# V turned by VectorE's 32x32 block transpose and read as strided weights, in a block of dilated attention and RG-LRU

## The chip, the core and the metric

The kernel runs on one core of a Trainium2 chip. Its engines work from queues of their own and wait for one another by semaphores: TensorE (PE; its weight loads are shown apart, as PEld), VectorE (DVE), ScalarE (ACT), GpSimd (POOL), and SyncE (SP), which issues most DMAs here. The metric is device time of one execution in microseconds (us), lower is better. Shown times are medians of several executions. The profile is of one execution.

## What is computed

One decoder block in float32, for 2048 positions and a model width of 1024. An input projection to 9216 columns feeds attention (24 heads of 64 in three groups with dilations 1, 4 and 16), a gated linear recurrence, and gates. The change concerns V, from the projection to the product of the attention weights with it:

```python
proj = x @ w_in[l] + b_in[l]
q, k, v, g_attn, u_lru, g_lru, gate_logits = jnp.split(proj, SPLIT_POINTS, axis=-1)
...
def to_blocks(t):          # positions regrouped by residue mod dilation, then blocks of 128
    t = t.reshape(B, M, dilation, H, Dh).transpose(0, 2, 1, 3, 4)
    return t.reshape(B, dilation, nb, BAND_BLOCK, H, Dh)
...
s = jnp.einsum('brnqhd,brnkhd->brnhqk', qb, kw) * (Dh ** -0.5)
...
p = jnp.exp(s - m)
o = jnp.einsum('brnhqk,brnkhd->brnqhd', p, vw)
```

A query block of 128 sees its own key block and the one before it; with dilation 16 there is one block for each residue. The results of the groups are combined, gated and projected, merged with the recurrence branch, projected again and normalised.

## The kernel before

The kernel has three stages, one after the other.

**Stage A, the projection.** The 72 column tiles of 128 are computed in pairs, each pair for one half of the positions at a time ("plan", 72 entries). Most pairs go through a scheme with seven block products instead of eight: `product(s, j)` (L622) issues 12 matmuls of 128x512 into one PSUM bank `q`, with weights split into a high part `h` and a low part `l`; `evacuate(s, j)` (L650) combines the banks on DVE, and `result` (L587) makes one 128x512 tile (128 columns of the projection by 512 positions, called chunk `c`) out of a bank and a partial sum. One product is one tick of the schedule. A loop over the ticks (L878) issues the product, the events due at this tick (weight loads, and the preparation of weights, four products ahead of their use in the first half of the plan and three in the second), and the next steps of "chains": generators that do what is left for one result tile, each step held back by `Ask` until a budget of engine time is there. The order on every engine is thus fixed when the program is built.

Twelve column tiles are V, for three groups `g` and four pairs of heads `hp`, so there are 48 tiles of V: 24 in the first half of the plan and 24 in the second. `v_chain` (L363) handles one tile. It lays positions on partitions: four 128x128 transposes on PE (`turn`, L367, tile `vtp`) are put into the middle of a later product, ACT copies the bank to `vs` and applies the sign that the seven-product scheme leaves on the second tile of a pair (L378), and SP stores it to DRAM (`v_scr`, L382 and L384). PSUM is divided into four banks `q`, two `t` for `vtp` and two `g` for the recurrence's gates.

**Stage B, the attention.** There are 12 units `u` (a pair of heads in a group; groups in the order 0, 2, 1). `qk_parts` and `v_parts` (L805) load a unit's q, k and V one unit ahead into one of two buffers; `v_parts` gives four parts of one 256 KB DMA each, with partition = key within its block. A loop runs over 48 groups of work, four for each unit: scores (L992, L998), softmax numerators on DVE and ACT (L1012, L1014), their transposes on PE (L1029), and `values` (L1046), whose matmuls (L1061) take 64 columns of V, one head, as weights. The two heads of a unit go to different halves of the output partitions, so they come in pairs. From the fifth group on, 12 matmuls of the recurrence's projection (L1231, tile `yb`) stand in each group; their weights `wl` and inputs `hx` are loaded by SP and split by POOL. DMAs on SP rotate over eight semaphores; an issue waits until the DMA eight places before it has landed.

**Stage C** is the two last projections and the layer norm.

The lines that matter below: L360 to L385 (`v_chain`), L583 (a result tile out of a bank), L630 (a product's bank), L670 (a partial sum), L805 to L822 (`v_parts`), L1046 to L1062 (`values`).

Of the kernel before, what the change touches and what calls it, by code (L numbers as in the profile page):

```python
# [15 lines left out]
P = 128  # L16
S = 2048
# [14 lines left out]
def hybrid_block_kernel(ctx: ExitStack, tc: tile.TileContext, a: dict, out: bass.AP):  # L32
# [16 lines left out]

    v_scr = [[dram.tile([S, P], F32, name=f"v_scr{g}{j}") for j in range(HP)] for g in range(3)]  # L50

# [307 lines left out]

    vs_free = [sl_p.tile([P, 520], F32, name=f"vs{j}")[:, 0:CH].rearrange("p (b f) -> p b f", b=4) for j in range(2)]  # L360
    tog = {"n": 0}

    def v_chain(vt, sgn, f, c):  # L363
        g, hp = divmod(f - FT_V, 4)
        st = {}

        def turn():  # L367
            tp = st["tp"] = ps.tile([P, 4, P], F32, tag="t", name=f"vtp{f}_{c}", bufs=2)
            for b in range(4):
                pe.transpose(tp[:, b, :], flat(vt)[:, b * P:(b + 1) * P], ident)  # L370
            give(vt)

        yield Ask(cond=lambda: tog["n"] < 2)
        tog["n"] += 1
        pe_later(2, turn)
        yield Ask(lag=3, cond=lambda: len(vs_free) > 0, ACT=.66)
        vs = vs_free.pop(0)
        act.activation(vs, st["tp"], AF.Copy, scale=sgn)  # L378
        tog["n"] -= 1
        yield Ask()  # L380
        if g == 0:
            sp.dma_start(v_scr[g][hp].rearrange("(p n) f -> p n f", p=P)[:, 4 * c:4 * c + 4], vs)  # L382
        else:
            sp.dma_start(v_scr[g][hp][c * CH:(c + 1) * CH].rearrange("(b p) f -> p b f", p=P), vs)  # L384
        vs_free.append(vs)  # L385

# [200 lines left out]
    def result(s, fi, c, bank, u):  # L587
# [34 lines left out]
    def product(s, j):  # L622
# [27 lines left out]
    def evacuate(s, j):  # L650
# [154 lines left out]
    def v_parts(u):  # L805
        g, hp = unit(u)
        src = v_scr[g][hp]

        def part(i):
            def fn():  # L810
                if u == 0 and i == 0:
                    AT_X["v"] = big("X4", [P, 2, 16, P], F32, "V")
                V = AT_X["v"][:, u % 2, 4 * i:4 * i + 4]
                if g == 0:
                    sp.dma_start(V, src.rearrange("(p n) f -> p n f", p=P)[:, 4 * i:4 * i + 4])
                elif g == 1:
                    sp.dma_start(V, src[i * CH:(i + 1) * CH].rearrange("(j r) f -> j r f", r=4))
# [228 lines left out]
    def values(js, tag="o"):  # L1046
        o = aps.tile([P, 4, P], F32, tag=tag, name=f"o{js[0]}", bufs=2 if tag == "s0" else 1)
        out = []
        for i, j in enumerate(js):
            u, n0 = divmod(2 * j, 16)  # L1050
            g, _ = unit(u)
            V = AT_X["v"][:, u % 2]
            ptb, _, los = st.pop(("t", j))
            for b in range(2):
# [3 lines left out]
                for x in range(lo // P, 2):  # L1058
                    kb = n if x else pv
                    for h, hs in enumerate((lo_, up_)):  # L1060
                        pe.matmul(o[hs, 2 * i + b, :], V[:, kb, 64 * h:64 * h + 64], ptb[:, b, 2 * h + x, :],  # L1061
                                  start=(x == lo // P), stop=(x == 1))  # L1062
# [598 lines left out]
```

## Time and profile before

| | us |
|---|---|
| median of 3 executions (2113.68 to 2114.83) | 2114.58 |
| span of the profiled execution | 2110.6 |
| stage A, until the last matmul of L639 | about 1451 |
| stage B, first score matmul to the last of L1061 | 1451 to 1774 |
| busy in the span: PE, PEld, DVE, ACT, POOL | 2092.4, 1713.1, 1645.0, 1212.7, 764.2 |

The span is from the first to the last instruction; a time of the table's first row holds some 4 us more, which lie around it. Busy time of PE counts matmuls that overlap once. In the views below a row of the timeline is: start in us, duration in us, engine, line, operation, output<-inputs, shapes, number of instructions merged, and in brackets the idle time before it with what ended it. A row of the groups has busy time in us, then the mean of one in ns, then idle time before it. A row of the windows has busy time for each engine with the number of instructions, the clock granted to TensorE, the mean busy share of the DMA engines and GB/s.

### The profile page before, as it was taken

Reading aid. Unit: us, or ns where it says so; the run is one execution under the profiler, and the core shown is the slowest. Engines: PE = TensorE matmul, PEld = TensorE weight load, DVE = VectorE, ACT = ScalarE, POOL = GpSimd, SP = SyncE. Lnnn points to the kernel's source line nnn. Section 1 sums busy time; section 2 is a strip of 40 time slices with the busy share of each in tenths; the row PEclk is TensorE's granted clock in tenths of the full one; section 3 lists DMA queues with packets and bytes.
Section 4 is the critical chain, followed back from the end, with each engine's and each line's share of the span. In section 5 each row is a group of like instructions: output and inputs, shape, how many; then the busy total and the mean of one; then the engine's idle time right before and its main releaser. Section 6 shows DMA issues by size and latency. Waiting matters only on the chain.

```text
span 2110.6 us, 35731 instructions
## 1 busy us (share of the span) xinstructions
PE 2092.4 (99%) x12069; PEld 1713.1 (81%) x12069; DVE 1645.0 (78%) x2937; ACT 1212.7 (57%) x2510; POOL 764.2 (36%) x685
## 2 busy tenths in 40 slices
PE   9999999999999999999999999999999999999998
PEld 7888888888888888888888888887888878788886
DVE  8878988989988868677777878875667776877667
ACT  6456556567567556677677787775666664321100
POOL 1544653653653301111111111112547678521120
PEclk9999999999999999999999999999999999999999
DMA  7876976886886866566665666669879886774431
GB/s 222 245 230 196 266 227 203 255 239 208 248 256 210 301 192 181 191 205 174 206 190 175 207 205 204 188 205 275 209 208 260 233 234 184 243 243 154 152 100 70
DMA packets 259205, 443.10 MB, mean 210 GB/s; under 512 B 65504, under 2 KB 92160, under 8 KB 255952
## 3 DMA queue, kind: packets, MB, share of 16 engines
q1 hardware_dynamic: 242384, 408.38, 62.0%
q0 software_dynamic: 11744, 23.54, 6.0%
q10 hardware_dynamic: 4896, 8.92, 1.1%
q8 instruction: 96, 1.57, 0.3%
q14 instruction: 85, 0.70, 0.1%
HBM read 289.74 MB, written 150.99 MB: 209 GB/s over the span
## 4 chain that ended last, share of the span: by engine, by line
PE 95%; DMA 2%; DVE 1%; POOL 1%; ACT 1%; issue 1%; SPq 0%; ACTq 0%; POOLq 0%; DVEq 0%
PE q L639 65%; PE yb L1231 6%; PE o L1061 3%; PE z L1536 3%; PE z L1537 3%; PE z L1538 3%; PE pt L1029 2%; PE s L998 2%; PE ya L1504 1%; PE ya L1503 1%; PE ya L1505 1%; PE g L500 1%; PE vtp L370 1%; PE s L992 1%; DMA war<-in_w_f_dram 1%
## 5 line engine op out<-in xcount | busy, mean ns | idle before, releaser
L639 PE MATMUL q<-xT,hS 128*128 128x512 f32 x1632 | 505.0, 391 | 0.1
L639 PE MATMUL q<-xT,l 128*128 128x512 f32 x1088 | 423.5, 389 | 0.0
L639 PE MATMUL q<-xB,hA 128*128 128x512 f32 x1344 | 418.0, 392 | 0.0
L639 PE MATMUL q<-xB,l 128*128 128x512 f32 x944 | 367.9, 390 | 0.0
L639 PEld LDWEIGHTS q<-xT,hS 128*128 128x128 f32 x1632 | 304.6, 188 | 65.0 <-issue 2.7
L639 PEld LDWEIGHTS q<-xB,hA 128*128 128x128 f32 x1344 | 250.7, 188 | 57.0 <-issue 5.8
L639 PEld LDWEIGHTS q<-xT,l 128*128 128x128 f32 x1088 | 204.3, 188 | 42.6
L240 POOL TENSOR_TENSOR sw<-sw,sin 128x512 f32<-128x512 f32 x96 | 156.8, 1639 | 166.2 <-ACT sw L329 94.7
L639 PEld LDWEIGHTS q<-xB,l 128*128 128x128 f32 x944 | 177.5, 188 | 37.2
L240 POOL TENSOR_TENSOR y<-y,h 128x512 f32<-128x512 f32 x28 | 38.8, 1386 | 384.1 <-DVE h L541 352.1
L1014 ACT ACTIVATE pb<-pb 128x192 f32<-128x192 f32 (+1 forms) x384 | 160.7, 422 | 26.5 <-DVE pb L1012 26.4
L639 PE MATMUL q<-xB,hS 128*128 128x512 f32 x544 | 169.0, 392 | 0.0
L639 PE MATMUL q<-xT,hA 128*128 128x512 f32 x544 | 167.8, 390 | 0.0
L284 ACT ACTIVATE hA<-wA 128x512 fp32r<-128x512 f32 x220 | 138.6, 636 | 28.5 <-DVE l L240 9.1
L1231 PE MATMUL yb<-hx,wl 128*128 128x512 f32 x576 | 148.9, 400 | 0.1
L284 ACT ACTIVATE hS<-S 128x512 fp32r<-128x512 f32 x170 | 108.6, 639 | 60.7 <-DVE S L240 47.3
L240 POOL TENSOR_TENSOR l<-wA,hA 128x512 fp32r<-128x512 f32 x68 | 107.8, 1585 | 91.4 <-ACT hA L284 60.9
L1231 PEld LDWEIGHTS yb<-hx,wl 128*128 128x128 f32 x576 | 104.8, 188 | 28.4 <-issue 5.6
L639 PEld LDWEIGHTS q<-xT,hA 128*128 128x128 f32 x544 | 101.9, 188 | 21.4 <-issue 0.4
L639 PEld LDWEIGHTS q<-xB,hS 128*128 128x128 f32 x544 | 101.2, 188 | 21.5 <-issue 1.1
L240 DVE TENSOR_TENSOR S<-S,wA 128x512 f32<-128x512 f32 x102 | 96.8, 949 | 11.5 <-DMA wA<-in_w_in_dram 7.9
L1507 POOL TENSOR_TENSOR me<-gA,me 128x512 f32<-128x512 f32 x30 | 47.7, 1607 | 157.6 <-DVE gA L1506 135.3
(213 smaller groups left out, 4325.4 us busy)
## 6 DMA issues: line engine op xcount, KB each, us to landing
wA<-in_w_in_dram SPq DMA_DIRECT2D x220, 256.0 KB
wl_scr<-l SPq DMA_DIRECT2D x102, 512.0 KB
l<-wl_scr SPq DMA_DIRECT2D x102, 512.0 KB
wS<-in_w_in_dram SPq DMA_DIRECT2D x102, 256.0 KB
wS<-in_w_in_dram POOLq DMA_DIRECT2D x68, 256.0 KB, 7.0
wlr<-in_w_f_dram SPq DMA_DIRECT2D x64, 256.0 KB
mg_scr<-y SPq DMA_DIRECT2D x59, 256.0 KB
v_scr<-vs SPq DMA_DIRECT2D x48, 256.0 KB
```

The source lines that it names most:

```text
L240: eng.tensor_tensor(out=out, in0=in0, in1=in1, op=op)
L284: act.activation(heads(h), heads(r, False), AF.Copy)
L639: pe.matmul(bank, w[:, ks], x[:, kk, xx], start=(first and i == 0), stop=(last and i == 11))
L998: pe.matmul(bank[h][es, b, 0:BW], q[hs, n * P + 64 * e:n * P + 64 * e + 64], k_[hs, at + 64 * e:at + 64 * e + BW], start=True, stop=True)
L1014: act.activation(pp, pp, AF.Exp, scale=-1.0, bias=mm, accum_out=ll)
L1029: pe.transpose(pt[e][:, b, 2 * h + x, :], pdata(p, h, c, c + P)[hs], ident[hs, hs])
L1061: pe.matmul(o[hs, 2 * i + b, :], V[:, kb, 64 * h:64 * h + 64], ptb[:, b, 2 * h + x, :], start=(x == lo // P), stop=(x == 1))
L1231: pe.matmul(YB["t"], w[:, a, k], hx(8 * c + k)[:, b], start=(hf == 0 and m == 0), stop=(hf == 1 and m == 11))
L1507: (dve if i in (6, 7) else pool).tensor_tensor(out=ME[c][:, f], in0=ga, in1=ME[c][:, f], op=ALU.add)
L1536: pe.matmul(z, mh[:, k], w[:, 0, hs], start=(k == 0), stop=False)
L1537: pe.matmul(z, mh[:, k], w[:, 1, hs], start=False, stop=False)
L1538: pe.matmul(z, ml[:, k], w[:, 0, hs], start=False, stop=(k == 7))
```

## The change

For a tile of V the four PE transposes, the PSUM bank and the ACT copy go. DVE turns the tile itself, with an instruction that transposes each 32x32 block; its operands are strided so that the positions of one block are those that belong together in the group's order. After it a partition stands for a quarter of the features and a position within its block, so `v_scr` gets another layout, `[4, 128, 512]`, and the load puts the quarters of the features side by side: `v_parts` now fills a quarter of V's partitions (32 keys of each block) at a time, with one DMA of 256 KB for a quarter in group 2, and four DMAs of 64 KB, with pieces of 512 bytes, in groups 0 and 1. The keys of a block then lie in V with a stride, of 64 bytes in group 2 and 16 bytes in the others, and `values` reads them so as weights. The sign that ACT applied is now put into the sums on DVE: for V pairs the partial sum `u3` is made with the other sign, and the result is bias + partial sum - bank. The two banks freed go to `q`, which has six. A buffer `vs` is given back two ticks later than before.

```diff
-    v_scr = [[dram.tile([S, P], F32, name=f"v_scr{g}{j}") for j in range(HP)] for g in range(3)]
+    v_scr = [[dram.tile([4, P, CH], F32, name=f"v_scr{g}{j}") for j in range(HP)] for g in range(3)]
...
-    def v_chain(vt, sgn, f, c):
+    def v_chain(vt, f, c):
+
         g, hp = divmod(f - FT_V, 4)
-        st = {}
-
-        def turn():
-            tp = st["tp"] = ps.tile([P, 4, P], F32, tag="t", name=f"vtp{f}_{c}", bufs=2)
-            for b in range(4):
-                pe.transpose(tp[:, b, :], flat(vt)[:, b * P:(b + 1) * P], ident)
-            give(vt)
-
-        yield Ask(cond=lambda: tog["n"] < 2)
-        tog["n"] += 1
-        pe_later(2, turn)
-        yield Ask(lag=3, cond=lambda: len(vs_free) > 0, ACT=.66)
+        y = flat(vt)
+        yield Ask(lag=0, cond=lambda: len(vs_free) > 0, DVE=.3)
         vs = vs_free.pop(0)
-        act.activation(vs, st["tp"], AF.Copy, scale=sgn)
-        tog["n"] -= 1
+        if g == 2:
+            dve.transpose(vs.rearrange("p (j r) -> p r j", r=16), y.rearrange("p (i r) -> p r i", r=16))
+        else:
+            src = y.rearrange("p (b q i) -> p q b i", q=4, b=4) if g == 0 else y.rearrange("p (q i b) -> p q b i", q=4, b=4)
+            dve.transpose(vs.rearrange("p (q j b) -> p q b j", q=4, b=4), src)
+        give(vt)
         yield Ask()
-        if g == 0:
-            sp.dma_start(v_scr[g][hp].rearrange("(p n) f -> p n f", p=P)[:, 4 * c:4 * c + 4], vs)
-        else:
-            sp.dma_start(v_scr[g][hp][c * CH:(c + 1) * CH].rearrange("(b p) f -> p b f", p=P), vs)
-        vs_free.append(vs)
+        if g == 2:
+            sp.dma_start(v_scr[g][hp][c], vs)
+        else:
+            sp.dma_start(v_scr[g][hp][:, :, P * c:P * c + P].rearrange("q p x -> p q x"), vs.rearrange("p (q x) -> p q x", q=4))
+        later(2, lambda: vs_free.append(vs))
...
-            total(flat(y), bank, u, f, sgn, True)
-            start_chain(qk_chain(y, f, c) if kind == "qk" else v_chain(y, sgn, f, c))
+            if kind == "v" and fi:
+                dve.scalar_tensor_tensor(out=flat(y), in0=u, scalar=b72[:, f:f + 1], in1=bank, op0=ALU.add, op1=ALU.subtract)
+            else:
+                total(flat(y), bank, u, f, sgn, True)
+            start_chain(qk_chain(y, f, c) if kind == "qk" else v_chain(y, f, c))
...
-            Q["b"] = ps.tile([P, CH], F32, tag="q", name=f"q{j}_{s}", bufs=4)
+            Q["b"] = ps.tile([P, CH], F32, tag="q", name=f"q{j}_{s}", bufs=6)
...
-            tt(dve, Q["u3"], Q["u2"], b, ALU.add)
+            if plan[s][4] == "v":
+                dve.scalar_tensor_tensor(out=Q["u3"], in0=b, scalar=-1.0, in1=Q["u2"], op0=ALU.mult, op1=ALU.subtract)
+            else:
+                tt(dve, Q["u3"], Q["u2"], b, ALU.add)
...
-        def part(i):
+        def part(q):
             def fn():
-                if u == 0 and i == 0:
-                    AT_X["v"] = big("X4", [P, 2, 16, P], F32, "V")
-                V = AT_X["v"][:, u % 2, 4 * i:4 * i + 4]
-                if g == 0:
-                    sp.dma_start(V, src.rearrange("(p n) f -> p n f", p=P)[:, 4 * i:4 * i + 4])
-                elif g == 1:
-                    sp.dma_start(V, src[i * CH:(i + 1) * CH].rearrange("(j r) f -> j r f", r=4))
+                if u == 0 and q == 0:
+                    AT_X["v"] = big("X4", [P, 2, 4, CH], F32, "V")
+                v = AT_X["v"][32 * q:32 * q + 32, u % 2]
+                m = src[q].rearrange("(a i) x -> i a x", a=4)
+                if g == 2:
+                    sp.dma_start(v, m)
                 else:
-                    sp.dma_start(V, src.rearrange("(i r) f -> i r f", r=16)[:, 4 * i:4 * i + 4])
+                    for c in range(4):
+                        sp.dma_start(v[:, c].rearrange("i (a x) -> i a x", a=4), m[:, :, P * c:P * c + P])
             return fn
...
             V = AT_X["v"][:, u % 2]
+            V = V.rearrange("p a (j r) -> p r (a j)", r=16) if g == 2 else V.rearrange("p c (f b) -> p c b f", b=4)
...
-                        pe.matmul(o[hs, 2 * i + b, :], V[:, kb, 64 * h:64 * h + 64], ptb[:, b, 2 * h + x, :],
+                        pe.matmul(o[hs, 2 * i + b, :], (V[:, kb] if g == 2 else V[:, kb // 4, kb % 4])[:, 64 * h:64 * h + 64], ptb[:, b, 2 * h + x, :],
                                   start=(x == lo // P), stop=(x == 1))
```

How the instructions move. On DVE, in stage A where the second pair of V column tiles leaves its banks (`q_7` are the products of that pair, `l_8` the low parts of weights prepared for the next), this stood in a row before:

```order
197 L240 TENSOR_TENSOR l_8_1709<-S_8_1688,hS_8_1738 128x4x2x64
198 L583 SCALAR_TENSOR_TENSOR y_0_1746<-q_7_1725,b_185,e_1649 128x512
199 L240 TENSOR_TENSOR vl_0_1766<-v_0_1639,vh_0_1765 128x512
200 L583 SCALAR_TENSOR_TENSOR y_0_1769<-q_7_1748,bn,v_1692 128x512
201 L240 TENSOR_TENSOR l_8_1763<-wS_8_1557,hS_8_1789 128x4x2x64
202 L583 SCALAR_TENSOR_TENSOR y_1_1797<-q_7_1771,b_185,u_1669 128x512
203 L240 TENSOR_TENSOR l_8_1819<-wA_8_1634,hA_8_1849 128x4x2x64
```

and this stands there now, on the same engine:

```order
201 L240 TENSOR_TENSOR l_8_1689<-S_8_1668,hS_8_1718 128x4x2x64
202 L577 SCALAR_TENSOR_TENSOR y_0_1726<-q_7_1705,b_185,e_1629 128x512
203 L240 TENSOR_TENSOR vl_0_1746<-v_0_1619,vh_0_1745 128x512
204 L372 STREAM_TRANSPOSE vs_212<-y_1_1702 128x4x4x32
205 L372 STREAM_TRANSPOSE vs_213<-y_0_1726 128x4x4x32
206 L595 SCALAR_TENSOR_TENSOR y_0_1751<-v_1672,b_185,q_7_1728 128x512
207 L240 TENSOR_TENSOR l_8_1743<-wS_8_1537,hS_8_1766 128x4x2x64
208 L577 SCALAR_TENSOR_TENSOR y_1_1776<-q_7_1753,b_185,u_1649 128x512
209 L240 TENSOR_TENSOR l_8_1793<-wA_8_1614,hA_8_1822 128x4x2x64
210 L240 TENSOR_TENSOR vl_1_1827<-v_1_1695,vh_1_1826 128x512
211 L372 STREAM_TRANSPOSE vs_212<-y_0_1751 128x4x4x32
212 L372 STREAM_TRANSPOSE vs_213<-y_1_1776 128x4x4x32
```

Two transposes now stand ahead of a low part of the weights, and two behind the next one; nothing else moved there.

On SP, where stage B begins (`qk` are the q and k of units 0 and 1, `V` those of unit 0 and then of unit 1, `wlr` and `hx` the inputs of the recurrence's projection), this was the order before:

```order
940 L800 DMA qk_13859<-q_scr_90 64x2048 x2
941 L800 DMA qk_13859<-k_scr_91 64x2048 x2
942 L815 DMA V<-v_scr_78 128x512 x4
943 L800 DMA qk_13937<-q_scr_106 64x2048 x2
944 L800 DMA qk_13937<-k_scr_107 64x2048 x2
945 L1181 DMA wlr_14029<-in_w_f_dram 128x512
...
947 L1202 DMA hx_13980<-hb_scr 128x512 x4
948 L819 DMA V<-v_scr_86 128x512 x4
```

and this is it now:

```order
940 L800 DMA qk_13619<-q_scr_90 64x2048 x2
941 L800 DMA qk_13619<-k_scr_91 64x2048 x2
942 L819 DMA V<-v_scr_78 32x4x128 x16
943 L800 DMA qk_13709<-q_scr_106 64x2048 x2
944 L800 DMA qk_13709<-k_scr_107 64x2048 x2
945 L1182 DMA wlr_13801<-in_w_f_dram 128x512
...
947 L1203 DMA hx_13752<-hb_scr 128x512 x4
948 L816 DMA V<-v_scr_86 32x4x512 x4
```

The sequence is the same, with 16 DMAs where there were four for a unit of group 0.

On PE, where the first tile of V was turned (`g_0` are the recurrence's gates), the first fence is before and the second now:

```order
292 L639 MATMUL q_4_1199<-xB_378,hS_4_1117 128x512 x2
293 L639 MATMUL q_4_1199<-xB_378,l_4_1119 128x512
294 L370 MATMUL vtp_1_1206<-ident,y_1_1153 128x128 x4
295 L500 MATMUL g_0_1211<-vh_0_1148,gw_0_1125 128x512
296 L500 MATMUL g_0_1212<-vh_0_1148,gw_0_1125 128x512
```

```order
292 L636 MATMUL q_4_1202<-xB_378,hS_4_1117 128x512 x2
293 L636 MATMUL q_4_1202<-xB_378,l_4_1119 128x512
294 L494 MATMUL g_0_1209<-vh_0_1148,gw_0_1125 128x512
295 L494 MATMUL g_0_1210<-vh_0_1148,gw_0_1125 128x512
296 L494 MATMUL g_0_1209<-vl_0_1149,gw_0_1125 128x512
```

The four transposes are gone, and the matmuls around them keep their places.

More of the change, by code (lines that the diff above doesn't have):

```diff
@@ L357, in qk_chain @@
         give_sent(rp)
[L360 to L363 removed]
+    vs_free = [sl_p.tile([P, 520], F32, name=f"vs{j}")[:, 0:CH] for j in range(2)]
+    def v_chain(vt, f, c):
         g, hp = divmod(f - FT_V, 4)
[L365 to L379 removed]
+        y = flat(vt)
+        yield Ask(lag=0, cond=lambda: len(vs_free) > 0, DVE=.3)
+        vs = vs_free.pop(0)
+        if g == 2:
[4 more added lines that the diff above has]
+        give(vt)
         yield Ask()
[L381 to L385 removed]
+        if g == 2:
+            sp.dma_start(v_scr[g][hp][c], vs)
+        else:
+            sp.dma_start(v_scr[g][hp][:, :, P * c:P * c + P].rearrange("q p x -> p q x"), vs.rearrange("p (q x) -> p q x", q=4))
+        later(2, lambda: vs_free.append(vs))
     def store_chain(t, dst):
```

## The prediction

> **What bounds the kernel now.** I read the page's head and its chain first, to see which engine sets the end; then what PE waits for; then the places where the change takes out, adds or lengthens something.
>
> ```profile
> span 2110.6 us, 35731 instructions
> ...
> PE 95%; DMA 2%; DVE 1%; POOL 1%; ACT 1%; issue 1%; SPq 0%; ACTq 0%; POOLq 0%; DVEq 0%
> PE q L639 65%; PE yb L1231 6%; PE o L1061 3%; PE z L1536 3%; PE z L1537 3%; PE z L1538 3%; PE pt L1029 2%; PE s L998 2%; PE ya L1504 1%; PE ya L1503 1%; PE ya L1505 1%; PE g L500 1%; PE vtp L370 1%; PE s L992 1%; DMA war<-in_w_f_dram 1%
> ```
>
> The reader is to see that the end is a sum of PE's work: 95% of the chain. The V transposes `vtp` stand in it with 1%, and the matmuls that read V, `o`, with 3%. The waits of PE say the same from the other side:
>
> ```profile
> PE first_bank L849 <- ACT warm L841: 3.2, 1, 3.2
> PE pt L1029 <- ACT ptb L1042: 2.3, 3, 1.5
> PE pt L1029 <- ACT pb L1014: 2.1, 2, 1.9
> ```
>
> These are the longest waits of PE in the whole span (total us, times, longest), and none is of L639, the projection. No product waits for a bank, so two more banks take away no wait; they can only soften a new one. The time around the span is 2114.58 - 2110.6 = 4.0 us, and I keep it.
>
> **What goes.** The chain in order of time, in a stretch with tiles of V:
>
> ```profile
> 204.84 5.67 PE q L639 x25
> 210.51 0.44 PE vtp L370 x4
> 210.94 2.76 PE q L639 x12
> 213.70 0.44 PE vtp L370 x4
> ```
>
> Four transposes hold PE for 0.44 us between two stretches of products that otherwise follow each other. There are 48 such groups: 48 x 0.44 = 21.1 us, all of it on the path. Their ACT copies go too; ACT is on 1% of the chain, so I count nothing for them. What is next in line when the 0.44 us go is the next product, whose weights are prepared four products (4 x 2.76 = 11 us) ahead in the first half of the plan; whether they still come in time is DVE's matter.
>
> **What DVE gets.** The trace has no DVE transpose. The nearest rows are single-input copies of the same 128x512 size, one with its output strided (unit 1, a stride of 64 bytes) and one without, and a two-input sum with strided output that ran beside POOL:
>
> ```profile
> 1487.54 1.05 DVE L1077 COPY o<-o 128x512 f32<-128x512 f32 x1
> 1541.94 0.69 DVE L1077 COPY o<-o 128x512 f32<-128x512 f32 x1
> 238.11 2.19 DVE L240 TENSOR_TENSOR rp<-y,sw 128x512 f32<-128x512 f32 x1
> ```
>
> So a transpose costs between 0.69 us and 2.19 us. I take 1.1, next to the strided copy, since every transpose writes with a stride of 16 bytes or more. That is 24 x 1.1 = 26.4 us in each half of the plan. The changed signs make six sums in each half a little longer, which I leave out beside it. Where V is made, DVE has this room:
>
> ```profile
> core 0: us, PE busy (x) PEld busy (x) DVE busy (x) ACT busy (x) POOL busy (x), PEclk, DMA share, GB/s
> 100.00:260.00 160.00, 160.00 (x731) 132.19 (x731) 137.80 (x161) 91.49 (x151) 83.13 (x62) 1.00 0.76 227
> 260.00:420.00 160.00, 160.00 (x731) 132.23 (x731) 138.50 (x161) 91.76 (x151) 83.83 (x63) 1.00 0.77 229
> ...
> 820.00:960.00 140.00, 140.00 (x648) 113.59 (x647) 100.46 (x146) 96.16 (x154) 22.20 (x16) 1.00 0.62 193
> 960.00:1120.00 160.00, 160.00 (x736) 130.16 (x735) 122.83 (x178) 111.70 (x181) 24.03 (x17) 1.00 0.63 195
> ```
>
> From 100 to 420 us DVE is busy for 276.3 of 320 us and idle for 43.7. The new work takes 26.4 of them, and PE, faster by 24 x 0.44 = 10.6 us, leaves that much less time: 43.7 - 26.4 - 10.6 = 6.7 us remain, 2%. In the second half 300 - 223.3 = 76.7 us are idle, which is ample. So DVE hides its work in the second half, and in the first nearly, but not evenly: the order on DVE shows pairs of transposes in front of low parts of weights, and where DVE has no idle time a pair makes all behind it 2.2 us late. That eats into the lead of 11 us and, with six banks, seldom stops a product. I count 4 us lost, of at most 10.6 (all that the first half gains) while a transpose stays under 43.7 / 24 = 1.8 us.
>
> **What the strided weights cost.** In stage B each load of weights takes 64 columns of V, one element per column and partition, now each in a place of its own 16 or 64 bytes on. No weight load in the trace is strided. What it may cost is bounded by what the loads hide behind:
>
> ```profile
> 1473.42 0.14 PEld L1061 LDWEIGHTS o<-ptb,V 128*64 128x64 f32 x2
> ...
> L1061 PEld LDWEIGHTS o<-ptb,V 128*64 128x64 f32 x1200 | 64.5, 137 | 3.3
> ...
> L992 PEld LDWEIGHTS s<-qk 64*128 64x128 f32 x336 | 20.8, 189 | 0.4 <-issue 0.4
> ...
> 1515.28 1.53 PE L998 MATMUL s<-qk 64*64 64x192 f32 x32
> ...
> 1517.39 1.97 PE L1061 MATMUL o<-ptb,V 128*64 128x128 f32 x32
> ...
> 1473.49 1.90 PE o L1061 x32
> ```
>
> The first row is the pair of loads for the two heads: two in 0.14 us, the duration of one, so they run side by side. 128 columns take 189 ns and 64 take 137, so 64 columns are some 52 ns of the load. The matmuls hold PE for 1.90 / 16 = 119 ns a pair. The score matmuls come in fours with the same 64 columns of weights and are 192 wide, and take 1.53 / 8 = 191 ns: about 192 / 128 of the pair's time. So the width of the moving operand sets the pace, not the load, and a load may grow from 52 to some 115 ns unseen. The DVE copy above paid (1.05 - 0.69) / 512 = 0.70 ns more per strided element; at that price a load takes 52 + 64 x 0.70 = 97 ns. Low end: nothing. High end: the two loads of a pair, no longer side by side, 2 x 97 = 194 ns instead of 119, 600 x 75 ns = 45 us. I take nothing, as both loads stay under the pair's time by the nearest strided row; the high end is a rival below. [...]
>
> **What the loads of V cost.** The same bytes come in 16 DMAs instead of four for the eight units of groups 0 and 1. Where stage B begins:
>
> ```profile
> 1440.37 1.78 SPq L815 DMA_DIRECT2D V<-v_scr  x4
> 1442.20 1.55 SPq L800 DMA_DIRECT2D qk<-q_scr  x2
> ...
> 1451.39 6.29 SPq L1202 DMA_DIRECT2D hx<-hb_scr  x4
> ...
> 1464.23 0.61 POOL L1206 CAST hx<-hx 128x512 fp32r<-128x512 f32 x1 [10.32 <-DMA hx<-hb_scr]
> ...
> 1474.49 1.28 POOL L1207 TENSOR_TENSOR hx<-hx 128x512 fp32r<-128x512 f32 x1
> 1475.32 0.50 PE L1231 MATMUL yb<-hx,wl 128*128 128x512 f32 x1
> ...
> 1451.00:1480.00 29.00, 25.86 (x420) 20.99 (x419) 21.32 (x103) 22.95 (x93) 15.98 (x19) 0.94 1.02 292
> ```
>
> Four issues take 1.78 us, so 12 more take 5.3 us, and behind them in SP's queue are q and k of unit 1, then `wlr` and `hx`. POOL waits for `hx` and then works without a gap until 1475.77, when PE has just begun its first `yb`: `hx` later by d makes PE wait for d less about 2 us. The DMA engines are full here (share 1.02), so part of SP's delay only empties their queue; I put d at 5 and the wait at 3 us. Between nothing and 5.3 us is possible. Further on there is room:
>
> ```profile
> 1480.76 1.06 SPq L817 DMA_DIRECT2D V<-v_scr  x2
> ...
> 1485.65 0.88 SPq L817 DMA_DIRECT2D V<-v_scr  x2
> ...
> 1510.23 1.53 PE L1061 MATMUL o<-ptb,V 128*64 128x128 f32 x24
> ...
> 1510.00:1600.00 90.00, 89.45 (x1184) 72.83 (x1180) 63.55 (x279) 61.06 (x253) 44.26 (x55) 1.00 0.80 218
> ```
>
> V of unit 2 is sent for by 1486.5 and first read at 1510.2; 5.3 us more do not reach PE, and DMA has a fifth of its time free. I count 1 us for what is pushed behind. [...]
>
> **The sum.** 2110.6 - 21.1 + 4 + 3 + 1 = 2097.5 for the span; with 4.0 around it 2101.5 us. With the ends of the costs that are not rivals (DVE 0 to 10.6, stage B 0 to 10) it lies between 2093.5 and 2110.
>
> **Rivals.**
>
> *The strided loads are not hidden.* Place: the 600 pairs of L1061. Price: 45 us, worked out above, from the point where the loads of a pair take more than 119 ns together. For it: two loads and two moving operands read the same partitions at once, and DVE's row shows that a stride costs. Against it: the loads run side by side now, and one alone stays under the limit. Time: 2101.5 + 45 = 2146.5 us, slower than before; between 2130 and 2180.
>
> *DVE becomes the bound.* With 2.19 us a transpose, the first half has 276.3 + 24 x 2.19 = 328.9 us of DVE work for 320 us: instead of gaining 10.6 us it loses 8.9, and instead of my 4 us of loss that is 19.5: 2101.5 + 15.5 = 2117 us. For it: long rows like 2.19 are common beside POOL. Against it: they have two inputs, a transpose has one.
>
> *The loads of V reach PE.* If in each of the seven later units of groups 0 and 1 a late `wlr` or `hx` stops PE for 2 us, 14 us go: 2115.5 us. For it: the DMAs on SP rotate over eight semaphores, so small ones shorten what is under way. Against it: the 24 us between load and use above.
>
> **Chances.** The forecast 0.62, the loads not hidden 0.18, DVE the bound 0.10, the V loads 0.10. The range must leave out no more than 0.2: from 2092, a little under the forecast's low end, to 2124, above the last two rivals; the first rival stays outside. A measurement can tell some 0.2% (4.2 us) from no change. Faster: nearly all of the forecast and some of the two small rivals, 0.65. Same, from 2110.4 to 2118.8: the greater part of those two, 0.13. Slower: the first rival and the rest, 0.22.
>
> **What would show it.** Right: no `vtp`; PE's projection ends about 17 us earlier, at about 1434; rows of the DVE transpose near 1.1 us; L1061 still at 1.90 us for 32; a gap of PE of a few us before its first `yb`. Wrong: waits of L639 for DVE between 100 and 420 us (DVE the bound); 32 matmuls of L1061 in 3 us (loads not hidden); PE waiting for POOL or DMA in each unit of stage B (the loads of V).

## The result, and the profile after

The changed kernel takes 2131.23 us (median of 4 runs, 2126.93 to 2134.10) against 2114.7 us: a ratio of 1.0077, with a 95% interval of 1.0061 to 1.0094. It is slower by 16.5 us where I forecast 13 us faster, and it lies above the range.

Head and chain of the page of the changed kernel:

```profile
span 2132.3 us, 35366 instructions
...
PE 59%; DMA 7%; DVE 2%; POOL 2%; ACT 2%; issue 1%; SPq 1%; POOLq 0%; DVEq 0%; ACTq 0%
PE q L636 37%; PE yb L1232 5%; PE z L1539 3%; PE z L1538 3%; PE z L1537 3%; PE o L1062 2%; DMA V<-v_scr 2%; DMA hx<-hb_scr 1%; PE pt L1029 1%; PE s L998 1%; PE ya L1505 1%; PE ya L1506 1%; PE ya L1504 1%; PE g L494 1%; POOL hx L1208 1%
```

`vtp` is gone from the chain, and `DMA V<-v_scr`, which wasn't there, has 2% of it. PE's 59% can't be set beside the 95% of before: the parts sum to 74%, so a quarter of this chain is missing (run rows, below, is as fast as the kernel before and has 37%). PE's waits say more; here are the longest totals (total us, times, longest):

```profile
PE w L1156 <- DMA wh<-w_scr: 7.8, 3, 5.7
PE pt L1029 <- ACT ptb L1042: 5.2, 3, 4.6
PE yb L1232 <- POOL hx L1208: 3.6, 5, 0.9
PE first_bank L849 <- ACT warm L841: 3.2, 1, 3.2
PE q L636 <- DVE l L240: 2.8, 4, 1.2
PE pt L1029 <- ACT pb L1014: 2.2, 2, 2.1
PE g L498 <- ACT tr L514: 2.1, 1, 2.1
PE q L636 <- ACT hS L284: 1.0, 1, 1.0
PE g L498 <- DVE vl L240: 1.0, 1, 1.0
```

Two kinds are new: in the projection (L636, L498) PE waits for DVE and for what follows DVE; in stage B it waits for `wh`, a small load of 24 KB, and for other things that come through SP's queue.

To place the loss I compared the start of the same matmul in both traces: the n-th product of the projection, the last matmul on V, the end. This table is worked out from the traces of one execution each; the first row is the kernel before in us, the others say how much earlier (-) or later (+) each kernel is there. A single execution can lie some us from the median: that of the changed kernel is the longest of its four (2134.10 us), that of rows_32 the shortest of its ten (2111.76 us, median 2117.89). The names are those of the experiments below.

```
                 proj.   proj.   proj.   proj.   last     span
                 #1728   #2304   #4896   end     V matm.
before           418.9   553.3   1171.0  1451.2  1774.6   2110.6
changed          -10.7    -3.5    -14.2   -12.3   +19.7    +21.7
q_four            -8.4    -1.1    -12.0    -8.8   +22.1    +23.7
act_copy          -6.5    -6.5    -18.3   -18.5   +11.4    +12.2
dense_transpose  -11.7    -5.3    -16.2   -15.1   +13.7    +16.4
contig_read      -11.2    -4.3    -14.2   -12.3   +14.9    +17.2
four_loads       -10.9    -3.2    -13.8   -11.8    +6.9    +10.2
four_contig      -10.2    -3.5    -13.4   -11.5    +8.2    +10.7
rows              -7.2    +1.3     -9.3    -7.4    +1.7     +4.3
rows_32           -7.6    -2.0    -11.9   -10.0    +0.4     -0.7
before_16         -0.8    -0.8     -0.8    -0.7   +29.0    +31.0
before_16_rows    -0.3    -0.3     -0.2    -0.2   +24.0    +27.5
before_4_pieces    0.0     0.0     +0.1    +0.1    +2.5     +3.4
half              -0.5    -0.5     -7.5    -7.5    -4.3     -5.8
```

Read the row of the changed kernel from left to right. While V is made (100 to 420 us) all the gain of the first 24 groups is there, 10.7 us. Then, with V done, 7.2 us are given back by 550 us. The second half gains 10.7 and gives back 1.9. The projection ends 12.3 us earlier, of 21.1 that went. From there to the end 34.0 us are lost. So stage B is the larger part, and the projection a smaller one.

Stage B, SP's queue. Five rows of its timeline in the kernel before, at the loads of V for one unit; then the same place of the changed kernel (start, length with the waits between the issues in it, line, number of DMAs):

```profile
1643.19 1.23 SPq L800 DMA_DIRECT2D qk<-k_scr  x2
1644.47 1.06 SPq L817 DMA_DIRECT2D V<-v_scr  x2
1645.62 0.85 SPq L1181 DMA_DIRECT2D wlr<-in_w_f_dram  x2
1646.57 1.03 SPq L817 DMA_DIRECT2D V<-v_scr  x2
1652.83 2.29 SPq L1148 DMA_DIRECT2D wh<-w_scr  x4
```

```profile
1644.35 1.23 SPq L800 DMA_DIRECT2D qk<-k_scr  x2
1645.62 11.00 SPq L819 DMA_DIRECT2D V<-v_scr  x8
1656.74 0.83 SPq L1182 DMA_DIRECT2D wlr<-in_w_f_dram  x2
1657.62 4.80 SPq L819 DMA_DIRECT2D V<-v_scr  x8
1662.54 1.61 SPq L1149 DMA_DIRECT2D wh<-w_scr  x4
```

PE at the same time, in its timeline in the changed kernel:

```profile
1657.28 2.35 PE L1232 MATMUL yb<-hx,wl 128*128 128x512 f32 x9
1665.33 0.77 PE L1156 MATMUL w<-wh,sel 128*128 128x512 f32 x1 [5.69 <-DMA wh<-w_scr]
```

The loads of V of one unit held SP for 11.00 + 4.80 = 15.8 us instead of 1.06 + 1.03 = 2.1. `wh` stands behind them, is sent for at 1662.5, and PE stands for 5.69 us. SP was not issuing for all of those 11 us: it waited. Its waits in stage B (1440 to 1780 us) name what for, in the kernel before and in the changed one. The line numbers stand for different loads: before, L815, L817 and L819 load V of groups 0, 1 and 2; now L819 loads groups 0 and 1, and L816 group 2.

```profile
SPq L819 <- DMA qk<-k_scr: 4.3, 2, 2.7
...
SPq L815 <- DMA qk<-k_scr: 1.4, 1, 1.4
```

```profile
SPq L819 <- DMA qk<-k_scr: 19.4, 14, 2.4
...
SPq L819 <- DMA qk<-q_scr: 14.3, 8, 2.3
...
SPq L819 <- DMA wlr<-in_w_f_dram: 5.6, 8, 1.0
```

So SP's waits for q, k and `wlr` at the loads of groups 0 and 1 go from 1.4 us to 39.3. In both traces SP's DMAs share eight semaphores in turn, and an issue mostly waited for the DMA eight before it, whose semaphore it takes over: of SP's waits for one of its own DMAs, 148 of 159 are for the one eight issues back in the changed kernel, and 121 of 131 in the kernel before. Eight loads of V in a row, right behind loads of q and k of 512 KB each, run into these.

### The profile page after: what moved, and what is told of

The parts are those of the page before. It is cut to its first block, busy times and chain, and to the rows that moved or that the text cites. A ratio compares the mean times of both kernels' runs of the same rounds, so it can differ in the third digit from the quotient of the medians.

```text
span 2132.3 us, 35366 instructions
## 1 busy us (share of the span) xinstructions
PE 2090.9 (98%) x11877; PEld 1708.6 (80%) x11877; DVE 1685.6 (79%) x2985; ACT 1189.0 (56%) x2462; POOL 763.3 (36%) x685
## 4 chain that ended last, share of the span: by engine, by line
PE 59%; DMA 7%; DVE 2%; POOL 2%; ACT 2%; issue 1%; SPq 1%; POOLq 0%; DVEq 0%; ACTq 0%
PE q L636 37%; PE yb L1232 5%; PE z L1539 3%; PE z L1538 3%; PE z L1537 3%; PE o L1062 2%; DMA V<-v_scr 2%; DMA hx<-hb_scr 1%; PE pt L1029 1%; PE s L998 1%; PE ya L1505 1%; PE ya L1506 1%; PE ya L1504 1%; PE g L494 1%; POOL hx L1208 1%
## 5 line engine op out<-in xcount | busy, mean ns | idle before, releaser
L636 PE MATMUL q<-xT,hS 128*128 128x512 f32 x1632 | 503.7, 390 | 0.0
L636 PE MATMUL q<-xT,l 128*128 128x512 f32 x1088 | 423.7, 389 | 2.8 <-DVE l L240 2.8
L636 PE MATMUL q<-xB,hA 128*128 128x512 f32 x1344 | 415.8, 391 | 0.3 <-ACT hA L284 0.3
L636 PE MATMUL q<-xB,l 128*128 128x512 f32 x944 | 367.3, 389 | 0.0
L636 PEld LDWEIGHTS q<-xT,hS 128*128 128x128 f32 x1632 | 305.5, 188 | 66.6 <-issue 3.3
L636 PEld LDWEIGHTS q<-xB,hA 128*128 128x128 f32 x1344 | 251.9, 188 | 56.6 <-issue 4.1
L636 PEld LDWEIGHTS q<-xT,l 128*128 128x128 f32 x1088 | 204.2, 188 | 47.0 <-DVE l L240 4.5
L240 POOL TENSOR_TENSOR sw<-sw,sin 128x512 f32<-128x512 f32 x96 | 155.9, 1629 | 157.8 <-ACT sw L329 87.1
L636 PEld LDWEIGHTS q<-xB,l 128*128 128x128 f32 x944 | 177.3, 188 | 37.1
L240 POOL TENSOR_TENSOR y<-y,h 128x512 f32<-128x512 f32 x28 | 39.7, 1416 | 384.0 <-DVE h L535 339.0
L636 PE MATMUL q<-xB,hS 128*128 128x512 f32 x544 | 167.7, 389 | 1.0 <-ACT hS L284 1.0
L636 PE MATMUL q<-xT,hA 128*128 128x512 f32 x544 | 167.9, 390 | 0.0
L240 POOL TENSOR_TENSOR l<-wA,hA 128x512 fp32r<-128x512 f32 x68 | 107.9, 1586 | 79.8 <-ACT hA L284 44.9
L636 PEld LDWEIGHTS q<-xB,hS 128*128 128x128 f32 x544 | 102.0, 188 | 22.8 <-ACT hS L284 1.4
L636 PEld LDWEIGHTS q<-xT,hA 128*128 128x128 f32 x544 | 101.9, 188 | 22.0 <-issue 1.1
L328 ACT ACTIVATE sw<-y 64x512 f32<-64x512 f32 x96 | 60.6, 631 | 79.4 <-DVE y L577 75.4
```

Source lines behind the costliest of these rows:

```text
L240: eng.tensor_tensor(out=out, in0=in0, in1=in1, op=op)
L328: act.activation(flat(sw)[lo_], flat(rw)[up_], AF.Copy, scale=scale)
L636: pe.matmul(bank, w[:, ks], x[:, kk, xx], start=(first and i == 0), stop=(last and i == 11))
```

## The experiments

Two theories at the start: (1) the number of DMAs on SP's queue is what stage B lost; (2) the transfers themselves are slow, by their 32 partitions. Besides these, the strided weights and DVE's load were to be priced. Times are medians, with the ratio to the runs of the kernel before on the same chip and its 95% interval.

**four_loads.** The scratch for V gets another order, so that a unit of groups 0 and 1 comes with 4 DMAs:

```
-    v_scr ... dram.tile([4, P, CH], ...)
+    v_scr ... dram.tile([4, P, CH] if g == 2 else [4, 4, P, P], ...)
-            sp.dma_start(v_scr[g][hp][:, :, P * c:P * c + P].rearrange("q p x -> p q x"), ...
+            sp.dma_start(v_scr[g][hp][:, c].rearrange("q p x -> p q x"), ...
-                    for c in range(4):
-                        sp.dma_start(v[:, c].rearrange("i (a x) -> i a x", a=4), m[:, :, P * c:P * c + P])
+                    sp.dma_start(v.rearrange("i c (a x) -> i (c a) x", a=4), src[q].rearrange("c (a i) x -> i (c a) x", a=4))
```

> The changed kernel, with V of groups 0 and 1 stored in four blocks of 64 KB a quarter so that it is loaded with 4 DMAs of 256 KB a unit (pieces of 512 bytes, 32 partitions as in the changed kernel) instead of 16 of 64 KB. Theory 1 (the number of DMAs on SP's queue is what stage B lost: SP stands before each of them until the DMA eight before it has landed, 5 to 11 us in each group of eight, and what is behind comes late): SP's waits at the V loads fall from 11 us in a group to under 3, the stops of PE in stage B between 1460 and 1760 us (about 25 us together) go, the pace of the matmuls that read V stays at 2.12 us for 32; time 2104 to 2112 us. Theory 2 (loads into 32 partitions are slow in themselves, or DMA as a whole is too full): it stays above 2122 us.

2121.1 us, 1.0030 (1.0018 to 1.0041): some 10 us better than the changed kernel, between the two forecasts. SP's waits at the V loads fall as theory 1 says, but from the end of the projection on 22.0 us are still lost (from -11.8 to +10.2). The number matters, and something else as well.

**contig_read.** The weights of L1062 from neighbouring addresses:

```
-            V = V.rearrange("p a (j r) -> p r (a j)", r=16) if g == 2 else V.rearrange("p c (f b) -> p c b f", b=4)
+            V = V.rearrange("p a (s f) -> p (a s) f", s=4) if g == 2 else V.rearrange("p c (b f) -> p c b f", b=4)
```

> The changed kernel, but the matmuls of L1062 take their 64 columns of weights from neighbouring addresses (so the attention's result is computed with wrong columns of V); transposes, stores and loads are as in the changed kernel. Theory 1 (strided weights cost 14 ns a pair, 2.12 against 1.90 us for 32 matmuls): L1062 back to 1.90 us for 32, weight loads of 137 instead of 209 ns, 600 pairs x 14 = 8.4 us less: about 2123 us. Rival A (the strided loads are the whole loss in stage B, through what they make late): 2098 us. Rival B (they are hidden and the slower pace has another cause): within 2 us of the changed kernel.

2131.7 us, 1.0089 (1.0074 to 1.0104), not to be told from the changed kernel. Yet the price of the stride is in the traces. The loads (groups) and a full set of matmuls (chain) in the changed kernel; then the same with neighbouring addresses, and PE's two longest waits there:

```profile
L1062 PEld LDWEIGHTS o<-ptb,V 128*64 128x64 f32 x1200 | 77.2, 208 | 3.5
```

```profile
1510.81 2.12 PE o L1062 x32
```

```profile
L1062 PEld LDWEIGHTS o<-ptb,V 128*64 128x64 f32 x1200 | 66.1, 139 | 3.6 <-issue 0.2
```

```profile
1508.78 1.90 PE o L1062 x32
```

```profile
PE w L1156 <- DMA wh<-w_scr: 10.0, 3, 5.2
PE pt L1029 <- ACT ptb L1042: 7.9, 3, 7.4
```

A load is 208 instead of 139 ns, 32 matmuls 2.12 instead of 1.90 us. Take it away and PE only waits longer, 10.0 and 7.9 us for `wh` and `ptb` instead of 7.8 and 5.2: in this kernel SP's queue and DMA set the pace of a part of stage B, and a slower PE is partly covered by that.

**before_16.** The kernel before with 16 loads:

```
+                    m = src.rearrange("(p n) f -> p n f", p=P)[:, 4 * i:4 * i + 4] if g == 0 else src[i * CH:(i + 1) * CH].rearrange("(j r) f -> j r f", r=4)
+                    for k in range(4):
+                        sp.dma_start(V[:, k], m[:, k])
```

> The kernel before, with V of groups 0 and 1 loaded with 16 DMAs of 64 KB a unit (one per block of 128 keys, all 128 partitions, the same pieces of 512 bytes) instead of 4 of 256 KB; nothing else. Theory 1 (the number of DMAs on SP's queue): 15 to 30 us slower than before, 2130 to 2145 us, with SP waiting at the V loads for the loads of q and k. Theory 2 (32 partitions, not the number): within 4 us of before.

2142.0 us, 1.0137 (1.0122 to 1.0152). Some 29 us, without a transpose moved and without a stride. As the next expectation says, I had misread the pieces: this run changed their size too.

**before_16_rows, before_4_pieces.** So the two were taken apart:

```
+                    for k in range(4):
+                        sp.dma_start(V[32 * k:32 * k + 32], m[32 * k:32 * k + 32])
```

```
+                    m = src.rearrange("(p k i) f -> p k i f", p=P, i=4) if g == 0 else src.rearrange("(k j i) f -> j k i f", k=4, i=4)
+                    sp.dma_start(AT_X["v"][:, u % 2].rearrange("p (k i) f -> p k i f", i=4)[:, :, i], m[:, :, i])
```

> The kernel before, V of groups 0 and 1 loaded with 16 DMAs of 64 KB a unit, but each of 32 partitions with whole rows of 2048 bytes, so that the number of DMAs changes and the piece does not. (The earlier run before_16 changed both: its pieces are 512 bytes, and those of the kernel before are 2048, not 512 as its expectation said.) Theory 1 (the number on SP's queue is the larger part): 15 us or more slower than before, 2128 us or more, with SP's waits at the V loads 20 us or more in all. Theory 3 (the pieces of 512 bytes, which take more time of the DMA engines for the same bytes): within 5 us of before.

> The kernel before, V of groups 0 and 1 loaded with 4 DMAs of 256 KB a unit over all 128 partitions, in pieces of 512 bytes (blocks i, i+4, i+8, i+12 in one DMA) instead of 2048. Theory 1 (the number): within 4 us of before. Theory 3 (the pieces): 10 us or more slower, 2123 us or more. If both work, 4 to 10 us slower, and before_16_rows 10 to 20.

16 DMAs of whole rows: 2139.6 us, 1.0120 (1.0101 to 1.0138). 4 DMAs of small pieces: 2115.5 us, 1.0002 (0.9992 to 1.0012). before_16 and before_4_pieces both load all 128 partitions in pieces of 512 bytes, and differ in the number of DMAs, and so in the bytes of each: 16 take 2142.0 us, 4 take 2115.5. The number makes this loss; the pieces over 128 partitions cost nothing that can be measured. before_16_rows by itself would not show it, since each of its DMAs also fills 32 partitions instead of 128; it shows that the loss comes with pieces of 2048 bytes too. SP's waits with 16 DMAs of rows in the kernel before:

```profile
SPq L817 <- DMA qk<-k_scr: 25.9, 16, 2.7
...
SPq L817 <- DMA qk<-q_scr: 7.6, 5, 2.1
...
SPq L817 <- DMA wlr<-in_w_f_dram: 6.8, 8, 1.6
```

They are the waits of the changed kernel, 40 us in all there as here.

**four_contig.** four_loads with the edit of contig_read.

> The kernel of four_loads, with the 64 columns of weights taken from neighbouring addresses (wrong columns of V, as in contig_read). If PE sets the pace again once SP and DMA hold it less, the 14 ns a pair come out of the time: 6 to 9 us under four_loads, 2112 to 2115 us. If stage B still goes by what DMA delivers, as contig_read showed for the changed kernel: within 3 us of four_loads.

2119.2 us, 1.0021 (1.0008 to 1.0034): within 3 us of four_loads, with PE again waiting more for `wh` (8.3 us instead of 4.0). By the rule of the expectation, stage B of four_loads still goes by DMA; the two intervals overlap.

**rows.** Four DMAs, all 128 partitions, pieces of 2048 bytes; the price is four stores instead of one for each tile of groups 0 and 1:

```
-            sp.dma_start(v_scr[g][hp][:, :, P * c:P * c + P].rearrange("q p x -> p q x"), vs.rearrange("p (q x) -> p q x", q=4))
+            for a in range(4):
+                sp.dma_start(v_scr[g][hp][:, c, P * a:P * a + P].rearrange("(q i) x -> i q x", q=4), vs[32 * a:32 * a + 32].rearrange("i (q x) -> i q x", q=4))
-                    for c in range(4):
-                        ...
+                    sp.dma_start(AT_X["v"][:, u % 2, q], src[:, q])
```

> The changed kernel with V of groups 0 and 1 stored by four DMAs of 64 KB a tile (one for each 32 partitions) into rows that lie as they will in the partitions, and loaded with 4 DMAs of 256 KB a unit over all 128 partitions in pieces of 2048 bytes; transposes, banks and strided weights as in the changed kernel. By theories 1 and 3 together stage B then loses only the strided weights (8 us) and a few: the start of stage C 2 to 8 us earlier than before, time 2104 to 2112 us. If 32 more stores in each half of the projection hold SP, the projection ends later than 1441 us. Rival (something else of the change holds stage B): above 2118 us.

2114.9 us, 1.0003 (0.9993 to 1.0013): 16 us won back, and no difference from the kernel before. It is 3 us above the forecast, which lies in the projection: its end is 4.9 us later than in the changed kernel (-7.4), and 2.3 us later in rows_32, which has the same stores, so the extra stores do cost there. In stage B, where PE now waits little, the strided weights show: from the end of the projection to the last matmul on V it loses 9.1 us, and the pace of the matmuls on V (L1060 there) is 2.12 us for 32. 600 pairs at (2.12 - 1.90) / 16 = 14 ns are 8.3 us.

**rows_32.** The same with loads by partitions:

```
-                    sp.dma_start(AT_X["v"][:, u % 2, q], src[:, q])
+                    sp.dma_start(AT_X["v"][32 * q:32 * q + 32, u % 2], src[32 * q:32 * q + 32])
```

> The kernel of rows, with the 4 loads of V a unit taken by 32 partitions (whole rows of 8192 bytes each) instead of by 2048 bytes of all 128 partitions. It asks what kept four_loads 6 us behind rows: its DMAs go to 32 partitions each, in pieces of 512 bytes. If loads into 32 partitions are slow in themselves: 4 us or more slower than rows, 2119 us or more. If it was the small pieces, or both only together: within 3 us of rows.

2117.9 us (2111.8 to 2122.8), 1.0018 (1.0008 to 1.0027): 3.0 us above rows, on the line between the two forecasts, its interval overlapping that of rows. What keeps four_loads behind rows stays open between 32 partitions, small pieces, and both.

**q_four.** `bufs=4` instead of 6 for the products.

> The changed kernel with four instead of six banks for products. Theory 1 (banks decide nothing, as in the kernel before, where no product waited for one): within 3 us of the changed kernel, projection ending at 1439 us within 2. Rival (the two banks hide part of DVE's lateness): the projection ends 3 us or more later, PE waiting for DVE or ACT to read a bank between 100 and 520 us.

2138.7 us, 1.0121 (1.0106 to 1.0136), above the interval of the changed kernel. I missed this one: the rival holds. The projection ends 3.5 us later, and PE waits 6.0 us for DVE's `u`, a sum that empties a bank. So the two banks are worth something beside DVE's load: 3.5 us here. The rest of the 7.5 us between the medians does not show in the two traces: from the end of the projection on q_four loses 32.5 us, the changed kernel 34.0.

**act_copy, dense_transpose.** The price of DVE's work, taken away and made smaller:

```
-            dve.transpose(vs.rearrange("p (q j b) -> p q b j", q=4, b=4), src)
+        act.activation(vs, y, AF.Copy)
```

```
-            dve.transpose(vs.rearrange("p (q j b) -> p q b j", q=4, b=4), src)
+        dve.transpose(vs, y)
```

> The changed kernel with each DVE transpose replaced by a copy of the same tile by ACT (so V isn't turned, and the attention takes wrong values); stores, loads and reads as in the changed kernel. It tells whose lateness takes 9 us from the projection behind the tiles of V (about 440 to 510 and 1170 to 1210 us). If it is DVE's 48 x 1.1 us: the projection ends at 1431 us within 2 (all 21 us of the groups of transposes gained) and the stops of PE for low weights from DVE between 440 and 510 us go. If it is something else that the change moved (ACT, the banks, the order): it ends at 1439 us within 2, as in the changed kernel. Stage B as in the changed kernel, so no time is forecast beyond that.

> The changed kernel with each DVE transpose reading and writing its tile without strides (so the values of V stand in other places, and the attention takes wrong ones). If the stride on the write makes it 1.107 us long, it takes about 0.69 us, as the unstrided copy does, and the projection ends 2 to 6 us before 1439 us, since DVE has 10 us less to do in the first half. If a transpose of this size takes 1.1 us whatever its strides, row and end stay as in the changed kernel within 1 us.

2124.7 and 2128.8 us, one run each. With no transposes on DVE the projection ends 18.5 us earlier than before instead of 12.3, and nothing is given back between 420 and 550 us: DVE's load took 6.2 of the 9 us. The other 2.6 are not explained; this run was behind by 420 us (6.5 us gained of 10.6), where PE waited 3.9 us for low parts of weights from DVE with no transpose there. Unstrided transposes end it at -15.1. Their rows, of the changed kernel and of this one:

```profile
L372 DVE STREAM_TRANSPOSE vs<-y 128x512 f32<-128x512 f32 x32 | 33.9, 1107 | 3.4 <-DMA v_scr<-vs 3.4
L369 DVE STREAM_TRANSPOSE vs<-y 128x512 f32<-128x512 f32 x16 | 17.0, 1107 | 0.0
```

```profile
L368 DVE STREAM_TRANSPOSE vs<-y 128x512 f32<-128x512 f32 x48 | 31.9, 692 | 4.6 <-DMA v_scr<-vs 4.4
```

**half.** Built from the findings: the first half of the projection and group 2 keep PE's transposes; 16 tiles go to DVE; rows in the scratch, 4 loads a unit, four banks:

```
+        if g == 2 or c < 2:
+            ... as in the kernel before ...
+        dve.transpose(vs.rearrange("p (q j b) -> p q b j", q=4, b=4), src)
+            for x in range(4):
+                sp.dma_start(v_scr[g][hp][:, c, P * x:P * x + P].rearrange("(q i) x -> i q x", q=4), ...)
```

> A version built from the findings: PE transposes stay in the first half of the projection, where DVE is full, and for group 2; the 16 tiles of groups 0 and 1 in the second half go to DVE. V of groups 0 and 1 is stored in rows that lie as they will in the partitions (four stores of 64 KB for each tile that DVE turns), and loaded with 4 DMAs of 256 KB a unit in pieces of 2048 bytes; four banks for products. By the theories: 16 x 0.44 = 7.0 us gained in the second half, less 1 or 2 us for DVE, less a third of 8.4 us for the strided weights: 2 to 4 us faster than before, about 2111 us. If 48 more stores, or anything else of the change, cost more than that: not faster than before.

2106.8 us (2106.0 to 2108.6), 0.9970 (0.9957 to 0.9982): faster than both, by 6.7 us against the kernel before where 2 to 4 were forecast. Its gain in the projection is 7.0 us, all that 16 groups give; stage B gives back 3.2 up to the last matmul on V, a third of the strided price and a little. Head and chain of its page, and PE's two longest waits after the first bank's:

```profile
span 2104.8 us, 35668 instructions
...
PE 95%; DMA 2%; DVE 1%; POOL 1%; issue 1%; ACT 0%; SPq 0%; ACTq 0%; DVEq 0%; POOLq 0%
```

```profile
PE pt L1056 <- ACT pb L1041: 2.1, 2, 1.9
PE pt L1056 <- ACT ptb L1069: 2.0, 3, 1.2
```

PE is the chain again, at 95%, and its waits for DVE in the projection and for `wh` are gone.

## Why the prediction was wrong

*What goes: right.* No `vtp`, and the two stretches where V is made gained 10.7 us each, against 21.1 forecast for both.

*DVE: right duration, loss too small.* I took 1.1 us; it is 1.107. I counted 4 us of loss in the projection and it was 9.1, inside the 10.6 that I had as the bound for the first half. Three windows of the changed kernel:

```profile
100.00:260.00 160.00, 159.40 (x705) 131.18 (x703) 140.29 (x167) 84.15 (x135) 83.40 (x63) 1.00 0.78 227
260.00:420.00 160.00, 159.45 (x704) 131.56 (x705) 148.76 (x183) 87.84 (x143) 85.08 (x63) 1.00 0.79 240
...
440.00:510.00 70.00, 65.90 (x279) 52.94 (x278) 64.78 (x75) 40.86 (x68) 32.46 (x26) 0.98 0.70 207
```

From 100 to 420 us DVE idles for 31.0 of 320 us, not for the 6.7 that I had worked out, and yet it is late. Two things were off. The sum of busy times was not a fixed bill: its two-input sums of L240 fell otherwise between POOL's work and became shorter, 170.9 us instead of 178.3. (In this window of the kernel before, 78 of them, beside which POOL worked for over 80% of their time, took 1220 ns in the mean, and 60, beside which it didn't work, 675; in the changed kernel these are 65 and 76.) That is about half of what DVE was busy less than I had counted (302.7 - 289.1 = 13.6 us); the rest is not traced. One group of the kernel before and of the changed one, in the same window:

```profile
L240 DVE TENSOR_TENSOR l<-wS,hS 128x512 fp32r<-128x512 f32 x16 | 27.6, 1727 | 7.6 <-ACT hS L284 7.6
```

```profile
L240 DVE TENSOR_TENSOR l<-wS,hS 128x512 fp32r<-128x512 f32 x16 | 20.6, 1288 | 6.4 <-ACT hS L284 6.3
```

And the lateness was paid at 440 to 510 us, where PE idles for 4.1 us and DVE is busy for 64.8 of 70. I did not look there, because my window ended with the last tile of V. The second half, which I called ample, paid 1.9.

*The strided weights: a cost that I put at nothing, at a fifth of the rival's price and not by its mechanism.* I put a strided load's part at 52 + 64 x 0.70 = 97 ns, under the pair's 119. Measured, a load grew by 208 - 137 = 71 ns, 1.1 ns a column, to an estimated 52 + 71 = 123 ns: a little over the limit that I had given, and the pair goes to 2.12 / 16 = 132 ns. The two loads of a pair did stay side by side (their starts are mostly 7 ns apart in both traces); 2 x 97 ns one behind the other, which the rival was priced by, did not come. So the term is 8.3 us, not nothing and not 45.

*The loads of V: this step failed.* "12 more take 5.3 us" priced the issues alone, and "I count 1 us for what is pushed behind" looked at V, which had 24 us in hand. Both missed that SP doesn't only issue: it waited for the DMA eight before, and these were mostly the loads of q and k (19.4 + 14.3 of the 39.3 us above). I had named the eight semaphores, as an argument for a rival at 14 us and 0.10, and then weighed against it the lead of V, not of `wh`, `wlr` and `hx` behind V. The kernel before with 16 DMAs a unit, and nothing else of the change, loses 26 us with pieces of 2048 bytes (before_16_rows) and 29 with pieces of 512 (before_16). At the start of stage B, where I put 3 us, about 5 were lost; the rest comes at later units.

*The sum.* For the projection I had 17.1 us earlier, and it was 12.3; from there on 4 us lost, and it was 34.0 in the profiled run. About 26 of these are the number of DMAs, by before_16_rows, and 8 the strides, by rows; contig_read shows that the two do not simply add, and in four_loads a loss stays that the number doesn't explain. The windows from the end of the projection to the last matmul on V, in the kernel before, the changed one and before_16_rows, say how the time went:

```profile
1451.20:1774.60 323.40, 318.17 (x4151) 258.98 (x4150) 229.19 (x987) 219.69 (x903) 213.62 (x259) 0.99 0.84 228
```

```profile
1438.90:1794.30 355.40, 335.40 (x4150) 273.71 (x4151) 229.34 (x987) 219.57 (x903) 213.35 (x259) 0.97 0.84 209
```

```profile
1451.00:1798.60 347.60, 327.08 (x4151) 264.16 (x4150) 229.27 (x987) 220.15 (x903) 213.62 (x259) 0.97 0.82 214
```

PE idles for 20.0 us in the changed kernel instead of 5.2, and is busy for 17.2 us more with the same matmuls. The strides are 8.3 of the 17.2. before_16_rows has no strides, and PE is busy for 8.9 us more there too, at a granted clock of 0.97 as in the changed kernel, against 0.99 in the kernel before; for two stops of the changed kernel the last section shows such slower work behind them. So I put the 32.0 us at about 15 of waiting, 8 of strides and 9 of slower work, an estimate from these windows.

I had treated the rivals as if one or the other came true. All three came at once: DVE and the strides at a part of their prices, the loads of V at nearly twice theirs (26 us instead of 14), and together they passed the top of the range. The sum has two slips besides. The high ends that I named give 2093.5 + 10.6 + 10 = 2114.1 us, not 2110; the 10 us for stage B were my estimate, which no run shows. And the 4.0 us around the span set the median of some executions against the span of another: in each run whose span is on record, the time is 1.7 to 2.2 us longer than the span. Neither is near the 30 us that were missed.

*Banks.* "No product waits for a bank, so two more banks take away no wait; they can only soften a new one" held in its second half: without them the kernel is 2138.7 us.

## What to carry to other kernels

When a load is cut into more DMAs, count what its queue waits for, not what an issue costs (here the loads of V for one unit held SP for 15.8 us instead of 2.1): look up which transfer stands as many places before it as the queue has semaphores, eight here, and check the lead of everything behind it, small loads first, as PE stood for 5.69 us for 24 KB of `wh`. Work moved to an engine that is nearly full can be paid after the stretch that made it, as 7.2 us were here between 419 and 553 us, so read the windows behind that stretch too. And where several cheap risks share a stage, price them together: the range should hold the case in which they all come true.

## What the runs showed of the hardware that was not expected

The two longest stops of PE in the changed kernel, of 5.69 and 4.62 us, were followed by slower work and cost more than their length. Windows around the one of 4.62 us at 1728 us (the columns as in the prediction, the granted clock third from the end):

```profile
1728.00:1733.00 5.00, 0.38 (x9) 0.19 (x6) 1.56 (x10) 1.06 (x3) 4.29 (x7) 0.83 1.00 292
1733.00:1738.00 5.00, 5.00 (x49) 4.55 (x50) 1.69 (x10) 3.61 (x17) 1.56 (x3) 0.50 1.05 272
1738.00:1744.00 6.00, 6.00 (x69) 5.17 (x68) 3.66 (x17) 2.27 (x11) 3.66 (x9) 0.99 0.49 120
```

After the wait the granted clock is 0.50 for about 5 us, in which 32 matmuls of L1062 take 3.63 us in the chain instead of 2.12. At half the clock 5 us hold work of 2.5, so the 4.6 us cost an estimated 7. The windows around the stop of 5.69 us at 1660 and around one of 1.48 us at 1757 show the lower clock behind the first and not behind the second:

```profile
1663.00:1670.00 7.00, 4.67 (x36) 3.84 (x36) 2.01 (x11) 0.95 (x4) 1.92 (x3) 0.51 0.66 188
...
1756.00:1764.00 8.00, 6.52 (x64) 5.12 (x63) 5.30 (x22) 4.14 (x20) 2.99 (x3) 1.00 0.72 220
```

Behind the first, 16 matmuls of L992 take 2.02 us instead of 1.11. None of my terms had this.

The strides made the transpose longer: 692 ns without (dense_transpose), 1107 ns with a stride on the write of 16 bytes (L372) or of 64 (L369), in both the same, (1107 - 692) / 512 = 0.81 ns an element. In group 0, which L372 has together with group 1, only the write is strided; in the other groups the read is too, and the transposes of L372 all took between 1055 and 1152 ns.
